# Hybrid decoder block on one core: the first inputs in single k steps behind products on constants, and sums of squares and cumulative sums as high and low parts in f32r

## The chip, the cores and the metric

One core of one Trainium2 chip runs the kernel: TensorE (matrix products), VectorE (DVE), ScalarE (ACT) and SyncE (SP), which issues the transfers. The metric is the device time in microseconds (us); before, the median of three runs is 1462.24 us (1460.91 to 1462.55).

## The reference

One layer of a hybrid decoder, for 256 positions (T) and a width of 2048 (D), all in float32. Cut to what matters:

```python
u = rmsnorm(h, g_mix_pre)                      # x * rsqrt(mean(x*x) + 1e-6) * g
proj = u @ w_in                                # q,k,v of 12 + 4 heads, two gates of width D
ya = dilated_mixture_attention(qa, ka, va) @ w_branch_a
yb = stick_breaking_attention(qb, kb, vb) @ w_branch_b
mix = (sigmoid(gla) * ya + sigmoid(glb) * yb) @ w_out
h = h + rmsnorm(mix, g_mix_post)
up = causal_depthwise_conv(rmsnorm(h, g_ffn_pre) @ w_up, conv_w, conv_b)
f = (gelu(up[:, :5632]) * up[:, 5632:]) @ w_down
h = h + rmsnorm(f, g_ffn_post)
out = h + sigmoid(h @ w_ple_gate) * (p @ w_ple_in)
```

Stick-breaking attention weighs key s for query t by `exp(z + ln + after)`, where `ln = log_sigmoid(-z)` and `after` is the sum of `ln` over the keys between s and t: an exclusive cumulative sum over up to 256 keys.

## The kernel before

Activations are held transposed: 16 tiles (k = 0 to 15) of 128 channels by 256 positions. The weights are packed on the host into one stream of tiles of 128x1024, eight blocks of 128x128 each, in the order in which TensorE uses them. A tile is loaded (`raw`, `NRAW` = 5 buffers), copied by ScalarE to f32r (`hi`, L147) and subtracted by VectorE (`lo` = `raw` - `hi`, L150); activations are split in the same way (`usplit`, `ulow`: the high part beside the low part in one tile of 512 columns). A block is then a pair of products in f32r (`mul`): the high weights by both parts (512 columns, L226), and the low weights by the high part (256 columns, L228). Sums and attention use plain f32 products.

`tick` runs once a tile: it issues deferred work (evacuations, squares), the copies of the tiles ahead (`high`, as far as `at["look"]` says) and the splits and further loads (`lows`). Each engine works in the order in which the program was written. All loads go through SP's queue; a load waits until its buffer's split (L150) is done.

What the change and the steps of the prediction touch:

- **The start.** The first group has four columns and takes k one after the other, so a k step needs one tile of x (128 KB) and half a weight tile (256 KB). The first two steps come singly, the rest of x by twos and the weights in whole tiles. Five weight tiles, w0 to w4, are asked for among x; w4 holds k = 8 and 9.
- **The norms of x and h** (`begin`). The products are not normalised: the norm's factor R is applied when a column is evacuated. Squares are summed beside the first six columns; then `total` multiplies the two sums by ones in f32 (L363), and `rstd` makes R.
- **Cumulative sums** (L520 to L522): ones-triangle `tri` and `allone` by `l1` in f32, once for each of the four head slots s.
- **The turns.** After the output projection (turn 0) and after the down projection (turn 1) the next projection needs h, and so R, first. `square_sum` adds the last column's square and splits the sum for two f32r products (L666), which stand after six of 16 blocks of the small e projection; the other ten blocks run while `rstd` makes R. Then h is updated by two tiles at a time: `scale` (times R, L674), `add` (to h, L678, and the high part on ScalarE), `rest` (the low parts). TensorE's first product of a step waits for the high part, and from the second step on for the low part too.

Of the kernel before, what the change touches and what calls it, by code (L numbers as in the profile page):

```python
# [14 lines left out]
T = 256  # L15
# [11 lines left out]
NRAW = 5  # L27
NSPL = 7
FIRST = 4
LATE = 2  # L30
SETTLE = dict(even=8, turned=9)
# [62 lines left out]
def hybrid_block_kernel(ctx: ExitStack, tc: tile.TileContext, gx, pT, convp, bias, masks, w, out):  # L94
# [161 lines left out]
    def mm(key, src, fn=mul, ps=None, even=0, turned=None):  # L256
# [110 lines left out]
    Rq = ab.tile([128, T], F32, name="Rq")  # L367
    mk = ab.tile([128, 5, 128], F32, name="mk")
    ident, keep01, neg, tri, allone = (mk[:, n] for n in range(5))
# [5 lines left out]
    parts = [(0, 1), (1, 2)] + [(k, k + 2) for k in range(2, KT, 2)]  # L375
    pieces = [[(0, NB // 2), (NB // 2, NB)], [(NB, 2 * NB)]]
    for n, (a, b) in enumerate(parts):
        o = 4 * KT if a else 0
        nc.sync.dma_start(gh[:, o + a * T:4 * KT + b * T], gx[:, o + a * T:4 * KT + b * T])
        if n < 2:  # L380
            for c, d in pieces[n]:
                load(0, c, d)
        elif a * NB // 1024 < NRAW:
            load(a * NB // 1024)
    at["load"] = NRAW
    DVE.memset(f(ones), 1.0)
    DVE.memset(eps32, EPS)
# [13 lines left out]
    usplit(u, 2, h[:, 2], gain(0, 2))  # L401
    at["high"] = at["low"] = 1
    at["look"] = 1
    for c, k, first, last in todo:
        if k == 6:
            at["grow"] = 0.5
        if c == 0 and 0 < k < KT - 2:
# [5 lines left out]
    nc.sync.dma_start(mk, masks)  # L413
    nc.sync.dma_start(cw, convp)

    def begin(pool, spare, keys, pss, src, act_src, name="sum"):
# [7 lines left out]
        pr = pool.tile([128, 2 * T], F32, name=name)  # L424
        total(pr, sq[:, 0], sq[:, 1])
        rstd(pr)

    def qk_evac(s, c, ps):
        def then(sum_to):
            st, r = (Q, Rq) if c < 4 else (K, R)  # L430
# [6 lines left out]
    begin(pat, spare, keys, pss, u, h, "z")  # L437
    DVE.tensor_scalar(Rq, R, 1.0 / math.sqrt(DH), None, op0=OP.mult)
    for c, ps in enumerate(pss):
        qk_evac(0, c, ps)  # L440
    for c in range(len(pss), 8):
        ps = mm(keys[c], u, ps=spare.pop(0) if spare else None)
# [28 lines left out]
    def attention(s):  # L471
# [31 lines left out]
        for c in (0, 256):  # L503
            DVE.tensor_tensor(l1[:, c:c + 128], l1[:, c:c + 128], keep01, OP.mult)
        yield
# [126 lines left out]
    def square_sum(last):  # L632

        sqs = tmp.tile([128, 2 * T], F32R, name="sqs", tag="s2", bufs=2)
        DVE.tensor_tensor(sq[:, 0], sq[:, 0], sq[:, 1], OP.add)
        s2 = square(last)
        DVE.tensor_tensor(sq[:, 0], sq[:, 0], s2, OP.add)
        ACT.activation(sqs[:, :T], sq[:, 0], AF.Copy)
# [237 lines left out]
```

## Time and profile before

| | |
|---|---|
| median of three runs | 1462.24 us |
| profiled execution | 1461.69 us |
| its span, from the first to the last instruction | 1459.9 us |
| TensorE busy | 1448.8 us, 99% of the span |
| VectorE busy, ScalarE busy | 1029.3 us (71%), 811.6 us (56%) |
| DMA engines, mean rate over the span | 60%, 188 GB/s |

A product's busy time runs over the next one's start, since products are pipelined; the step from one start to the next is what a product costs. The page's row of the clock granted to TensorE says 9 tenths or more in all 40 slices. In the rows further down "x4" puts together rows of the same instruction; an f32 product is recorded as two of them. What stands in brackets is the engine's idle time ahead of the instruction, and who ended it.

### The profile page before, as it was taken

The numbers are of one execution on the slowest core, as the hardware profiler recorded it, in microseconds if no ns is written. First come the engines' busy times: TensorE is split into PE (matmuls) and PEld (weight loads), VectorE is DVE, ScalarE is ACT, GpSimd is POOL, SyncE is SP. The second block draws the span as 40 slices with busy tenths as digits, with TensorE's granted clock in tenths as the row PEclk, the third lists the DMA queues.
The fourth block names the chain that finished last, engine by engine and source line by source line (L and its number), as shares of the span: only waits on it lengthen the run. The fifth ranks groups of instructions, "written<-read, shape, count | busy, mean of one in ns | idle before, by whom it ended". The sixth has DMA issues, their size and how long they took to land.

```text
span 1459.9 us, 21906 instructions
## 1 busy us (share of the span) xinstructions
PE 1448.8 (99%) x8433; PEld 1279.9 (88%) x8433; DVE 1029.3 (71%) x1533; ACT 811.6 (56%) x1217; POOL 0.2 (0%) x4
## 2 busy tenths in 40 slices
PE   8999999999999999999999999999999999999998
PEld 7888888889989998988888888888888888888888
DVE  7665555566666665698975787767877678778784
ACT  7463535365555456566754556545655456567562
POOL 0000000000000000000000000000000000000000
PEclk9999999999999999999999999999999999999999
DMA  8645555556666666635766666666666666666381
GB/s 325 223 155 181 171 192 169 193 176 194 188 188 188 188 188 188 221 126 169 214 208 189 189 189 196 189 188 189 188 192 194 190 188 188 189 195 209 114 264 54
DMA packets 78295, 275.11 MB, mean 188 GB/s; under 512 B 8688, under 2 KB 11632, under 8 KB 78192
## 3 DMA queue, kind: packets, MB, share of 16 engines
q1 hardware_dynamic: 78192, 273.73, 60.0%
q8 instruction: 66, 1.08, 0.3%
q14 instruction: 37, 0.30, 0.1%
HBM read 271.60 MB, written 2.10 MB: 187 GB/s over the span
## 4 chain that ended last, share of the span: by engine, by line
PE 98%; DVE 1%; DMA 0%; ACT 0%; SPq 0%; issue 0%
PE mm L226 55%; PE mm L228 29%; PE mm L464 2%; PE mm L462 2%; PE mm L463 2%; PE mm L247 2%; PE mm L246 2%; PE mm L245 2%; PE S L481 1%; PE S L226 1%; DMA raw<-in_w 0%; PE po L535 0%; PE S L515 0%; PE S L228 0%; PE po L226 0%; PE po L539 0%
## 5 line engine op out<-in xcount | busy, mean ns | idle before, releaser
L226 PE MATMUL mm<-u,hi 128*128 128x512 f32 x2596 | 906.2, 393 | 1.4 <-DVE u L318 1.4
L150 DVE TENSOR_TENSOR lo<-raw,hi 128x1024 fp32r<-128x1024 f32 (+1 forms) x506 | 613.3, 1218 | 173.6 <-ACT hi L147 166.1
L228 PE MATMUL mm<-u,lo 128*128 128x256 f32 x2578 | 722.3, 280 | 0.4 <-DVE lo L150 0.4
L147 ACT ACTIVATE hi<-raw 128x1024 fp32r<-128x1024 f32 (+1 forms) x506 | 530.7, 1053 | 244.2 <-PE mm L226 197.6
L226 PEld LDWEIGHTS mm<-u,hi 128*128 128x128 f32 x2596 | 485.8, 188 | 107.1 <-issue 1.6
L228 PEld LDWEIGHTS mm<-u,lo 128*128 128x128 f32 x2578 | 488.0, 189 | 1.8 <-DVE lo L150 0.9
L226 PE MATMUL mm<-ft,hi 128*128 128x512 f32 x693 | 240.4, 391 | 0.0
L273 ACT ACTIVATE t<-mm 128x256 f32<-128x256 f32 x242 | 91.4, 378 | 237.8 <-PE mm L228 237.5
L228 PE MATMUL mm<-ft,lo 128*128 128x256 f32 x693 | 194.0, 280 | 0.0
L276 DVE TENSOR_TENSOR s<-mm,t 128x256 f32<-128x256 f32 x211 | 88.9, 421 | 123.1 <-ACT t L273 123.1
L226 PEld LDWEIGHTS mm<-ft,hi 128*128 128x128 f32 x693 | 129.6, 187 | 28.4
L228 PEld LDWEIGHTS mm<-ft,lo 128*128 128x128 f32 x693 | 131.0, 189 | 0.0
L226 PE MATMUL mm<-mg,hi 128*128 128x512 f32 x240 | 83.2, 391 | 0.0
L228 PE MATMUL mm<-mg,lo 128*128 128x256 f32 x239 | 66.9, 280 | 0.0
L742 ACT ACTIVATE cv<-cpad,cw 128x256 f32<-128x256 f32 x88 | 52.6, 597 | 10.4 <-DVE cpad L737 10.2
L226 PEld LDWEIGHTS mm<-mg,hi 128*128 128x128 f32 x240 | 44.8, 187 | 9.7
L462 PE MATMUL mm<-hi,u 128*128 128x512 f32 x128 | 51.2, 400 | 0.0
L464 PE MATMUL mm<-hi,u 128*128 128x512 f32 x128 | 50.0, 391 | 0.0
L463 PE MATMUL mm<-lo,u 128*128 128x512 f32 x128 | 49.8, 389 | 0.0
L228 PEld LDWEIGHTS mm<-mg,lo 128*128 128x128 f32 x239 | 45.2, 189 | 0.0
L746 DVE SCALAR_TENSOR_TENSOR cv<-cpad,cw,cv 128x256 f32<-128x256 f32 x88 | 42.6, 485 | 3.1
L745 DVE SCALAR_TENSOR_TENSOR cv<-cpad,cw,cv 128x256 f32<-128x256 f32 x88 | 42.1, 478 | 0.0
(183 smaller groups left out, 1003.0 us busy)
## 6 DMA issues: line engine op xcount, KB each, us to landing
raw<-in_w SPq DMA_DIRECT2D x507, 512.0 KB, 3.7
bi<-in_bias SPq DMA_DIRECT2D x4, 576.0 KB, 4.6
out<-t SPq DMA_DIRECT2D x16, 128.0 KB, 3.8
gh<-in_gx SPq DMA_DIRECT2D x7, 256.0 KB, 7.0
mk<-in_masks SPq DMA_DIRECT2D x1, 320.0 KB, 5.2
raw<-in_w SPq DMA_DIRECT2D x2, 128.0 KB, 2.5
raw<-in_w SPq DMA_DIRECT2D x1, 256.0 KB, 4.1
t<-in_pT SPq DMA_DIRECT2D x2, 128.0 KB, 5.0
```

The lines of the kernel that those rows point to most:

```text
L147: ACT.activation(hi[i][:, a:b], raw[i][:, a:b], AF.Copy)
L150: DVE.tensor_tensor(lo[i][:, a:b], raw[i][:, a:b], f(hi[i][:, a:b]), OP.subtract)
L226: PE.matmul(ps, wh, rhs, start=first, stop=last, skip_group_check=True)
L228: PE.matmul(ps[:, :T], wl, rhs[:, :T], start=False, stop=last, skip_group_check=True)
L273: ACT.activation(t1[0], ps[:, T:], AF.Copy)
L276: DVE.tensor_tensor(out, ps[:, :T], t1[0], OP.add)
L462: PE.matmul(pv[t], xh, wh, start=kt == 0, stop=False)
L463: PE.matmul(pv[t], xh, wl, start=False, stop=False)
L464: PE.matmul(pv[t], xl, wh, start=False, stop=kt == KT - 1)
L742: ACT.activation(y, c[:, 2:], AF.Identity, scale=cw[:, n, 2:3], bias=cw[:, n, 3:4])
L745: DVE.scalar_tensor_tensor(y, c[:, 1:T + 1], cw[:, n, 1:2], y, op0=OP.mult, op1=OP.add)
L746: DVE.scalar_tensor_tensor(y, c[:, 0:T], cw[:, n, 0:1], y, op0=OP.mult, op1=OP.add)
```

## The change

1. **Start.** x and the weights of the first eight k steps come in pieces of one step (`EARLY` = 8), each piece split as it comes; then x by twos, and only then w4. Raw buffers are four instead of five. Six f32 products of 128 columns on a tile of ones (`WARM` = 6), into a bank that nothing reads, stand ahead of TensorE's first product, and the two fills of constants come ahead of the loads.
2. **Sums of squares.** All go through `halves`: a copy to f32r on ScalarE and a subtraction on VectorE, and `total` is then two f32r products. In `begin`, sum and `rstd` move from the end of the sixth column to after three blocks of the seventh (`mid`).
3. **Cumulative sums.** `l1` is split in the same way (`l2`), `tri` is copied to f32r, and the products are two of 384 columns and two of 128.
4. **Turns.** The sum is in two parts: squares of columns 0 to 14 (after three blocks of e) and of column 15 (after five in turn 0, after six in turn 1). The first of these is added and split ahead of `lows`, which stood first before. The first two tiles of h are scaled and added one by one, and their low parts come ahead of the next tiles' scaling.

On SP's queue the start reads so before (L379 loads x, L119 weights; the first x transfer has the gains in it, 512 columns of x are two k steps and 1024 columns of weights are one tile):

```order
L379 DMA gh<-in_gx 128x320
L119 DMA raw<-in_w 128x256 x2
L379 DMA gh<-in_gx 128x256
L119 DMA raw<-in_w 128x512
L379 DMA gh<-in_gx 128x512
L119 DMA raw<-in_w 128x1024
L379 DMA gh<-in_gx 128x512
L119 DMA raw<-in_w 128x1024
L379 DMA gh<-in_gx 128x512
L119 DMA raw<-in_w 128x1024
L379 DMA gh<-in_gx 128x512
L119 DMA raw<-in_w 128x1024
```

After it come three more of x, and then weights. Now, from step 5 on (the rows of steps 1 to 4 repeat in pairs):

```order
L400 DMA gh<-in_gx 128x256
L121 DMA raw<-in_w 128x512
L400 DMA gh<-in_gx 128x256
L121 DMA raw<-in_w 128x512
L400 DMA gh<-in_gx 128x256
L121 DMA raw<-in_w 128x512
L400 DMA gh<-in_gx 128x512 x4
L121 DMA raw<-in_w 128x1024 x9
```

The first five transfers are the same; w4, fifth of the whole tiles before and ahead of x's last three transfers, is now the first of the nine that stand behind all of x.

On VectorE, at the end of the down projection (turn 1), before (L150 splits a weight tile, L331 adds a square, L784 adds the last column, L635 to L639 make the sum and its low part, L674 scales, L678 adds to h):

```order
L150 TENSOR_TENSOR lo<-raw,hi 128x1024
L331 TENSOR_TENSOR sq<-sq,t 128x256
L784 TENSOR_TENSOR ff<-ff,mm 128x256
L635 TENSOR_TENSOR sq<-sq 128x256
L637 TENSOR_TENSOR sq<-sq,t 128x256
L639 TENSOR_TENSOR sqs<-sq,sqs 128x256
L353 TENSOR_SCALAR ms<-sum 128x256
```

and now (L336 adds a square, L379 and L369 make the first sum and its low part, L152 splits the weight tile, L817 adds the last column, L369 makes its square's low part):

```order
L336 TENSOR_TENSOR sq<-sq,t 128x256
L379 TENSOR_TENSOR sq<-sq 128x256
L369 TENSOR_TENSOR sp<-sq,sp 128x256
L152 TENSOR_TENSOR lo<-raw,hi 128x1024
L817 TENSOR_TENSOR ff<-ff,mm 128x256
L369 TENSOR_TENSOR sp<-t,sp 128x256
L358 TENSOR_SCALAR ms<-sum 128x256
```

The weight tile's split has moved from ahead of the last square's add to behind it and the two new operations; the last column's add still follows it.

The same engine after R in turn 1, before:

```order
L674 TENSOR_TENSOR ts<-ff,R 128x512
L678 TENSOR_TENSOR gh<-gh,ts 128x512
L674 TENSOR_TENSOR ts<-ff,R 128x512
L316 TENSOR_TENSOR u_12682<-gh,u_12682 128x256 x2
L678 TENSOR_TENSOR gh<-gh,ts 128x512
```

and now (L708 and L709 are the same on one tile, L321 the low parts):

```order
L708 TENSOR_TENSOR ts<-ff,R 128x256
L709 TENSOR_TENSOR gh<-gh,ts 128x256
L708 TENSOR_TENSOR ts<-ff,R 128x256
L709 TENSOR_TENSOR gh<-gh,ts 128x256
L321 TENSOR_TENSOR u_12730<-gh,u_12730 128x256 x2
L700 TENSOR_TENSOR ts<-ff,R 128x512
L704 TENSOR_TENSOR gh<-gh,ts 128x512
```

The first tile is ready for its high part after two short operations instead of two long ones, and the low parts (x2) stand ahead of the next scaling instead of behind it.

The diff, cut to its core:

```diff
-NRAW = 5
+NRAW = 4
+EARLY = 8
+WARM = 6
...
         for n, (_, k, first, last) in enumerate(group(key)):
+            if n == 3 and mid:
+                mid()
...
-    def total(ps, *accs, start=True, stop=True):
-        for n, acc in enumerate(accs):
-            PE.matmul(ps[:, :T], f(ones), acc, start=start and n == 0, stop=stop and n == len(accs) - 1)
+    def halves(src):
+        sp = tmp.tile([128, 2 * T], F32R, name="sp", tag="s2", bufs=2)
+        ACT.activation(sp[:, :T], src, AF.Copy)
+        DVE.tensor_tensor(sp[:, T:], src, f(sp[:, :T]), OP.subtract)
+        return sp
+    def total(ps, sp, start=True, stop=True):
+        for n in range(2):
+            PE.matmul(ps[:, :T], ones, sp[:, n * T:(n + 1) * T], start=start and n == 0, stop=stop and n == 1)
+    def sum_squares():
+        DVE.tensor_tensor(sq[:, 0], sq[:, 0], sq[:, 1], OP.add)
+        return halves(sq[:, 0])
...
-    parts = [(0, 1), (1, 2)] + [(k, k + 2) for k in range(2, KT, 2)]
-    pieces = [[(0, NB // 2), (NB // 2, NB)], [(NB, 2 * NB)]]
+    parts = [(k, k + 1) for k in range(EARLY)] + [(k, k + 2) for k in range(EARLY, KT, 2)]
+    pieces = {k: [(k // 2, k % 2 * NB + c, k % 2 * NB + d)
+                  for c, d in ([(0, NB // 2), (NB // 2, NB)] if k == 0 else [(0, NB)])] for k in range(EARLY)}
...
+    for _ in range(WARM):
+        PE.matmul(spare[2][:, :128], f(ones), f(ones), start=True, stop=True)
-    for k in range(2):
+    for k in range(EARLY):
         usplit(u, k, h[:, k], gain(0, k), low=False)
-        for c, d in pieces[k]:
-            high(0, c, d)
-            low(0, c, d)
-        ulow(u, k, h[:, k], gain(0, k))
+        k and ulow(u, k, h[:, k], gain(0, k))
+        for piece in pieces[k]:
+            high(*piece)
+            low(*piece)
+        k or ulow(u, k, h[:, k], gain(0, k))
...
-        PE.matmul(ps[:, 0:256], tri, l1[:, 0:256], start=True, stop=False, skip_group_check=True)
-        PE.matmul(ps[:, 128:256], allone, l1[:, 256:384], start=False, stop=True, skip_group_check=True)
-        PE.matmul(ps[:, 256:384], tri, l1[:, 256:384], start=False, stop=True, skip_group_check=True)
+        for c in range(2):
+            PE.matmul(ps[:, :384], tri, l2[:, c], start=c == 0, stop=c == 1, skip_group_check=True)
+        for c in range(2):
+            PE.matmul(ps[:, 128:256], ones, l2[:, c, 256:], start=False, stop=c == 1, skip_group_check=True)
...
     ps = mm(("down", NQ - 1, KT - 1), ft, mul1)
+    flush()
+    sps = [sum_squares()]
     lows(at["high"])
-    flush()
     DVE.tensor_tensor(ff[:, KT - 1], ff[:, KT - 1], ps[:, :T], OP.add)
-    sqs = square_sum(ff[:, KT - 1])
+    sps.append(halves(square(ff[:, KT - 1])))
...
-            if i == 5:
-                for c in range(2):
-                    PE.matmul(pr[:, :T], ones, sqs[:, c * T:(c + 1) * T], start=c == 0, stop=c == 1)
+            if i in (2, 4 + half):
+                total(pr, sps[i > 2], i == 2, i > 2)
...
         def add(n):
-            DVE.tensor_tensor(h[:, k:k + 2], h[:, k:k + 2], ts.pop(n), OP.add)
+            if n:
+                DVE.tensor_tensor(h[:, 2 * n:2 * n + 2], h[:, 2 * n:2 * n + 2], ts[n], OP.add)
+            for j in range(2):
+                k = 2 * n + j
+                if n == 0:
+                    DVE.tensor_tensor(ts[0][:, j], src[:, k], R, OP.mult)
+                    DVE.tensor_tensor(h[:, k], h[:, k], ts[0][:, j], OP.add)
                 usplit(dst, k, h[:, k], gn[k], low=False)
...
         add(0)
+        rest(0)
         scale(1)
-        rest(0)
         add(1)
```

## Rows read from the trace of the kernel before

**Rows 1.** The page: the chain that ended last, by engine.

```profile
PE 98%; DVE 1%; DMA 0%; ACT 0%; SPq 0%; issue 0%
```

**Rows 2.** Timeline of the first 22 us, TensorE: start us, us, engine, line, operation.

```profile
3.90 0.58 PE L235 MATMUL mm<-u,hi 128*128 128x256 f32 x1 [3.90 <-ACT hi L147]
...
9.40 0.63 PE L226 MATMUL mm<-u,hi 128*128 128x512 f32 x1
...
10.04 0.63 PE L226 MATMUL mm<-u,hi 128*128 128x512 f32 x1
...
13.87 0.40 PE L226 MATMUL mm<-u,hi 128*128 128x512 f32 x1
...
14.22 0.40 PE L226 MATMUL mm<-u,hi 128*128 128x512 f32 x1
...
21.29 0.40 PE L226 MATMUL mm<-u,hi 128*128 128x512 f32 x1
```

**Rows 3.** Start: VectorE, ScalarE (same columns), SP's waits, the page's weight loads.

```profile
7.39 0.69 DVE L150 TENSOR_TENSOR lo<-raw,hi 128x512 fp32r<-128x512 f32 x1 [1.67 <-ACT hi L147]
...
9.97 1.06 ACT L147 ACTIVATE hi<-raw 128x1024 fp32r<-128x1024 f32 x1 [0.89 <-DMA raw<-in_w]
...
18.88 1.06 ACT L147 ACTIVATE hi<-raw 128x1024 fp32r<-128x1024 f32 x1 [1.32 <-DMA raw<-in_w]
...
19.98 1.23 DVE L150 TENSOR_TENSOR lo<-raw,hi 128x1024 fp32r<-128x1024 f32 x1 [1.11 <-ACT hi L147]
...
SPq L119 <- DMA raw<-in_w: 2.2, 3, 0.9
...
raw<-in_w SPq DMA_DIRECT2D x507, 512.0 KB, 3.7
```

**Rows 4.** The chain in order of time, sums of squares: start us, us.

```profile
44.07 0.86 PE z L363 x4
...
621.33 0.25 PE sum L666 x2
```

**Rows 5.** Timeline, the first cumulative sum: start us, us.

```profile
103.84 0.59 PE L520 MATMUL z<-l,mk 128*128 128x256 f32 x2
...
104.27 0.38 PE L521 MATMUL z<-l,mk 128*128 128x128 f32 x2
...
104.49 0.39 PE L522 MATMUL z<-l,mk 128*128 128x128 f32 x2
```

**Rows 6.** Timeline of turn 0.

```profile
623.94 0.69 DVE L674 TENSOR_TENSOR ts<-mix,R 128x512 f32<-128x512 f32 x1
...
625.95 0.39 PE L235 MATMUL mm<-u,hi 128*128 128x256 f32 x1 [0.79 <-ACT u L310]
...
628.00 0.89 DVE L318 SCALAR_TENSOR_TENSOR u<-gh,u 128x256 fp32r<-128x256 f32 x2
...
628.90 0.39 PE L226 MATMUL mm<-u,hi 128*128 128x512 f32 x1
```

**Rows 7.** Timeline of turn 1.

```profile
1357.70 1.23 DVE L150 TENSOR_TENSOR lo<-raw,hi 128x1024 fp32r<-128x1024 f32 x1 [0.44 <-ACT hi L147]
...
1357.97 0.40 ACT L322 ACTIVATE t<-ff 128x256 f32<-128x256 f32 x1
...
1358.84 0.42 DVE L331 TENSOR_TENSOR sq<-sq,t 128x256 f32<-128x256 f32 x1
...
1359.61 0.42 DVE L784 TENSOR_TENSOR ff<-ff,mm 128x256 f32<-128x256 f32 x1 [0.35 <-PE mm L247]
...
1360.07 0.42 ACT L322 ACTIVATE t<-ff 128x256 f32<-128x256 f32 x1 [1.15 <-DVE ff L784]
...
1361.42 0.42 DVE L639 TENSOR_TENSOR sqs<-sq,sqs 128x256 fp32r<-128x256 f32 x1 [0.48 <-ACT sqs L638]
...
1366.58 0.39 PE L235 MATMUL mm<-u,hi 128*128 128x256 f32 x1 [0.70 <-ACT u L310]
...
1369.54 0.39 PE L226 MATMUL mm<-u,hi 128*128 128x512 f32 x1
```

More of the change, by code (lines that the diff above doesn't have):

```diff
@@ L374, in hybrid_block_kernel @@
     NB = FIRST * 128
-    parts = [(0, 1), (1, 2)] + [(k, k + 2) for k in range(2, KT, 2)]
-    pieces = [[(0, NB // 2), (NB // 2, NB)], [(NB, 2 * NB)]]
-    for n, (a, b) in enumerate(parts):
+    parts = [(k, k + 1) for k in range(EARLY)] + [(k, k + 2) for k in range(EARLY, KT, 2)]
+    pieces = {k: [(k // 2, k % 2 * NB + c, k % 2 * NB + d)
+                  for c, d in ([(0, NB // 2), (NB // 2, NB)] if k == 0 else [(0, NB)])] for k in range(EARLY)}
+    DVE.memset(f(ones), 1.0)
+    DVE.memset(eps32, EPS)
+    for a, b in parts:
         o = 4 * KT if a else 0
         nc.sync.dma_start(gh[:, o + a * T:4 * KT + b * T], gx[:, o + a * T:4 * KT + b * T])
-        if n < 2:
-            for c, d in pieces[n]:
-                load(0, c, d)
+        if a < EARLY:
+            for piece in pieces[a]:
+                load(*piece)
         elif a * NB // 1024 < NRAW:
@@ L413, in hybrid_block_kernel, with begin @@
     nc.sync.dma_start(mk, masks)
+    defer((None, None), (None, None), (lambda: ACT.activation(tri, mk[:, 3], AF.Copy), None))
     nc.sync.dma_start(cw, convp)
-    def begin(pool, spare, keys, pss, src, act_src, name="sum"):
+    def begin(pool, spare, keys, pss, src, act_src, then, name="sum"):
         at["grow"] = 1
@@ L423, in begin, with mid @@
         flush()
-        pr = pool.tile([128, 2 * T], F32, name=name)
-        total(pr, sq[:, 0], sq[:, 1])
-        rstd(pr)
+        sp = sum_squares()
+        def mid():
+            pr = pool.tile([128, 2 * T], F32, name=name)
+            total(pr, sp)
+            rstd(pr)
+            then()
+        return mid
     def qk_evac(s, c, ps):
         def then(sum_to):
-            st, r = (Q, Rq) if c < 4 else (K, R)
+            st, r = (Q, Rs[1]) if c < 4 else (K, R)
             if c % 4 == 0:
@@ L436, in hybrid_block_kernel, with then @@
     keys = [("qk", 0, c) for c in range(8)]
[L437 to L440, printed above, removed]
+    def then():
+        Rs.append(tmp.tile([128, T], F32, name="Rq", tag="y"))
+        DVE.tensor_scalar(Rs[1], R, 1.0 / math.sqrt(DH), None, op0=OP.mult)
+        for c, ps in enumerate(pss):
+            qk_evac(0, c, ps)
+    mid = begin(pat, spare, keys, pss, u, h, then, "z")
     for c in range(len(pss), 8):
-        ps = mm(keys[c], u, ps=spare.pop(0) if spare else None)
+        ps = mm(keys[c], u, ps=spare.pop(0) if spare else None, mid=mid if c == len(pss) else None)
         qk_evac(0, c, ps)
@@ L630, in scaled @@
         return lambda: ACT.activation(src[:, j], src[:, j], AF.Copy, scale=gain(gi, j)), None
[L632 to L638, printed above, removed]
-        DVE.tensor_tensor(sqs[:, T:], sq[:, 0], f(sqs[:, :T]), OP.subtract)
-        return sqs
     for j, ps in enumerate(several("out", 3, mg, 1)):
@@ L646, in hybrid_block_kernel @@
     ps = mm(("out", KT - 1), mg, mul1)
+    flush()
+    sps = [sum_squares()]
     lows(at["high"])
-    flush()
-    sqs = square_sum(ps[:, :T])
+    sps.append(halves(square(ps[:, :T])))
     DVE.tensor_scalar(mix[:, KT - 1], ps[:, :T], gain(1, KT - 1), None, op0=OP.mult)
@@ L652, in hybrid_block_kernel, with turn @@
     fp_sc, fp = scope("fp")
-    def turn(half, edst, sqs, src, gnext, dst, nxt):
+    def turn(half, edst, sps, src, gnext, dst, nxt):
         at["hold"] = True
@@ L846, in _arrays @@
     a["masks"] = np.ascontiguousarray(np.stack([
-        i == j, i < j, np.where(i < j, 0.0, NEG), i >= j, np.ones((128, 128))], 1).astype(np.float32))
+        i == j, i < j, np.where(i < j, 0.0, NEG), i >= j], 1).astype(np.float32))
     ws = {"w_in": w_in[0], "w_branch_a": w_branch_a[0], "w_branch_b": w_branch_b[0], "w_out": w_out[0],
```

42 lines of the change are left out of this document (22 added, 20 removed).

## The prediction

> **What bounds the kernel now.** I read the page's chain of waits first [rows 1]: 98% of that chain is TensorE itself. So the time is the sum of TensorE's products plus the few places where it stands still or runs slowly, and a change is worth only what it does to these. VectorE and ScalarE matter where TensorE waits for them: in the first 22 us, and in the two "turns", where a layer norm stands between two projections.
>
> Then the timeline of the first 30 us. A pair of products (512 and 256 columns) starts every 0.64 us at 9.40 and 10.04, but every 0.35 us at 13.87 and 14.22 [rows 2]. The page's clock row says full clock in every slice, so the level is read from the spacing: 1.2 GHz until about 13.4 us, 2.4 GHz after it, with TensorE at work since 3.9 us but with pauses. The ninth step of the first group (k = 8) starts at 21.29.
>
> Then the chain and timeline at the sums and cumulative sums [rows 4, 5], and around the two turns [rows 6, 7].
>
> **The change part by part.** Durations are of the profiled execution, which took 1461.69 us, of which 1459.9 are the span; the median of the three runs, 1462.24, is 0.55 us higher. What I sum goes on 1461.69; a median needs 0.55 more.
>
> *Start.* New are six products on constants before the data is there, and x and the weights in pieces of one k step for the first eight steps. The products on constants have no other reader, and before's TensorE is idle until 3.9 us [rows 2], so they cost nothing as long as they end by then: six f32 products of 128 columns at twice the 0.22 us of one at full clock [rows 5] are 2.6 us from about 1.0, so until 3.6. What they give is an earlier rise of the clock. How much of it reaches the end is decided by the fifth weight tile (w4, for k = 8). Before, it was asked for ahead of half of x. Now SP asks for w4 behind all of x and four tiles, so it lands with the 4640 KiB that x, the gains and five tiles make up. Before, 1568 KiB were there at 9.97 and 5152 KiB at 18.88, the two places where ScalarE waited for a transfer [rows 3]: 3584 KiB in 8.91 us, 402 KiB per us. 4640 KiB are there at 18.88 - 512/402 = 17.6, if the smaller pieces come at the same rate; I take 18.0 (estimate, a little for the shorter rows). From landing to the low part VectorE starts 1.10 us later and takes 1.23 [rows 3]: 20.35, so the first low product of k = 8 starts at 20.4. Before, it follows the one at 21.29 by 0.23, at 21.52. That is 1.1 us. The products before it are not later than that: the second step cannot start before about 8.1 us (it needs the same first five transfers, and before its split runs from 7.39 for 0.69 [rows 3]), and 28 pairs from there end at 17.9 at 0.35, and at 20.3 if the clock rises only at 13.4. So the clock's rise is largely hidden behind w4: TensorE gets to k = 8 early and waits there. Bounds of this term: 0 if w4 lands at 19.1, and 3.4 if nothing but TensorE counts (17.9 against 21.29). I take 1.1, from the nearest row.
>
> *Sums of squares.* Two f32 products of 256 columns take 0.86 us at the first of two such sums, and the second is alike; the same in f32r take 0.25 [rows 4]. Twice 0.61 is 1.2 us gained. New are an add, a copy and a subtraction, at 0.46 us a step [rows 7] some 1.4 us; they lie beside the products of the running column, and the sum now waits until three pairs (1.06 us) of the next column are through. If that cover were gone TensorE would wait 0.3 us.
>
> *Cumulative sums*, one per s, four in all. Before: 0.43 + 0.22 + 0.22 = 0.87 us [rows 5]. After: two products of 384 columns and two of 128 in f32r. 256 columns take 0.12 [rows 4], 512 take 0.35 - 0.12 = 0.23 [rows 2], so 384 take 0.175. A narrow f32r product is in no row. The bounds are 0.06 (half of 256) and 0.22 (the f32 product of 128 columns); nearest is the f32r one of 256, so I take 0.12. That is 0.35 + 0.24 = 0.59, a gain of 0.28, four times 1.1 us; by the bounds 0.3 to 1.6. The copy and the subtraction that split the operand lie beside the products of one attention step, several us before they are read.
>
> *First turn* (0, after the output projection). R comes 0.12 us earlier, since the final sum moves one block of three products (0.36) ahead and one pair of sums (0.24) comes in front of it. Tile 0 is now scaled, added and split by halves, so the first product can start 0.65 us earlier than 625.95 [rows 6]: the wait of 0.79 us nearly goes. But the same VectorE now does four operations of 256 where two of 512 stood, at steps of 0.46 where one needs the last one's result and 0.34 where not (0.42 less the 0.09 by which VectorE starts ahead of an end, as 1358.84 follows 1357.70 with its 1.23 [rows 7]) against 0.69 each, and does the low parts of tile 0 ahead of the next scaling. The low part that k = 2 needs started at 628.00 and now starts at about 628.4, while TensorE would be there at 628.25; with 0.5 us from there to the product it starts at 628.94, against 628.90. The wait is moved, not removed: 0, with bounds of 0.6 us gained and 0.3 lost.
>
> *Second turn* (1, after the down projection). Here an order changes for the worse. Before, VectorE splits the last weight tile at 1357.70, while it waits for ScalarE's square of 1357.97, and is free when the last column of the projection arrives at 1359.61 [rows 7]. Now the square's add, the new add and the new subtraction stand ahead of that 1.23 us split, and the last column's add stands behind it. Steps: add of the square 1358.39, sum 1358.85, copy on ScalarE 1359.31, subtraction 1359.76, split 1360.10, and 1.14 later (1357.70 to 1358.84) the last column's add, 1361.24 instead of 1359.61. From there square, copy and subtraction (0.46, 0.44, 0.45; one step fewer than before) end the chain with a subtraction at 1362.59, against 1361.42: R is 1.17 us later. The halves of tile 0 give 0.5 back, so the first product is at 1367.2 instead of 1366.58; and as in the first turn the low part for k = 2 is the next thing late, at 1370.3, its product at 1370.75 instead of 1369.54. That is a loss of 1.2 us, with bounds of 0.5 and 1.7.
>
> *Four raw buffers instead of five.* A tile takes 3.7 us to land, 1.06 to copy and 1.23 to split [rows 3], 6.0 us; four buffers cover four tiles of eight pairs, 11.3 us. Nothing, unless transfers take over 9 us.
>
> Sum: -1.1 - 1.2 - 1.1 + 0 + 1.2 = -2.2 us: 1459.5 on the profiled execution's time, 1460.0 as a median. A measurement of this kernel can tell about 0.2%, 2.9 us, from no change, so this is no change, with a lean towards faster.
>
> **The rivals.**
> 1. The start is bounded by TensorE: transfers keep up, w4 is there by 17.9. For it: the fast rate comes only after 8 us, and before's tiles were there before they were needed. Against it: 4640 KiB in all must be there, and w4 is the last of them. Start -3.4, the rest as above: -4.5, so 1457.7.
> 2. Smaller pieces come slowly (the other side). SP waited for the landing of earlier transfers before it issued new ones [rows 3], so the number in flight is limited; pieces half as large put half the bytes in flight. If the rate goes with the size, the twelve pieces of steps 2 to 7 (2304 KiB) at 201 KiB per us take 11.5 us from 6.7 (0.7 ahead of the split at 7.39), to 18.2, and x's rest with w4 (1536 KiB at 402) 3.8, to 22.0; the first low product of k = 8 is at 24.4, 2.9 us later than before. Sum +1.8, so 1464.0. The start loses from where w4 lands after 19.1, and from 20.2 on the whole is slower. Against it: half the bytes in flight are still 1.5 MiB, nearly 4 us of the measured rate.
> The Trainium skill, "DMA: Bandwidth & Descriptors", section Measured, speaks for this rival: it advises batching to 1 MiB or more for three quarters of the peak, with 138 GB/s at 64 KB and 341 at 1 MB. No run here shows a long row of 128 and 256 KB transfers, so it is not borne out yet.
> 3. The second turn is not delayed: the split of the last tile finds a gap, or TensorE's remaining products of that stretch cover it. Then the halves are worth what they are meant to be: 0 instead of +1.2, so -3.4 and 1458.8. Against it: VectorE works in order, and the split stands ahead of the add in its program.
>
> **How the numbers follow.** My forecast 0.53 (own range 1458.9 to 1461.6), rival 1 0.18, rival 2 0.10, rival 3 0.19. Faster by over 0.2% are rival 1, most of rival 3 and the low edge of mine (narrow products at 0.06, w4 at 17.6): 0.37. Slower by over 0.2% is only the far end of rival 2: 0.04. Within 0.2%: 0.59. The range runs from rival 1 to just past no change: 1457.6 to 1462.5.
>
> **What would show it.** Start: the first low product of k = 8 at 20.4, TensorE idle ahead of it, and pairs at 0.35 well before 13.4. If k = 8 starts at 18, rival 1; after 21.5, rival 2. Sums: two products at 0.25. Cumulative sums: z at 0.59 in place of 0.87; at 0.79 the narrow ones go at the f32 price. First turn: first product near 625.3 on before's scale, then a pause before k = 2. Second turn: a weight split on VectorE between the halves and the last column's add, the second pair of sums waiting some 1.2 us, and pauses before k = 0 and k = 2. I am wrong if the second turn is no later than before, or if the time is under 1457.6 or over 1462.5.

## The result, and the profile after

The changed kernel takes 1465.49 us (median of ten runs, 1464.17 to 1465.82); the kernel before, run beside it, 1461.34 (1460.85 to 1462.55). The ratio is 1.0025, with a 95% interval of 1.0016 to 1.0035. It is slower by about 4 us where I had forecast 1460.0 and a lean towards faster; on 1461.34 instead of 1462.24 that forecast would have been 0.9 lower still. The profiled execution took 1465.45 us with a span of 1463.6, 3.7 more than before's.

To see where these 3.7 us arise I set each of the 3577 products of L226 (512 columns, now L228) against the same product in the trace of before and followed the difference in their starts. It is -1.6 us at 41.8, +3.9 at 52.6 (just behind the first sum), +2.0 at 311 (behind the four cumulative sums), +2.3 behind the first turn, +1.8 behind the second sum, +3.0 behind the second turn and +3.5 from 1395 to the end. One place, the first sum, lost 5.6 us. All else together gained 2.0, of which the four cumulative sums are 1.4.

The page's chain of waits is TensorE's as before, one point less [rows 1], and one point in 100 is over 14 us, so it can't show a loss of this size:

```profile
PE 97%; DVE 1%; DMA 1%; ACT 1%; SPq 0%; issue 0%; DVEq 0%; ACTq 0%
```

**The start**, TensorE in the timeline (start us, us, engine, line, operation, idle time ahead of it and what ended it), answering to [rows 2]:

```profile
1.04 2.93 PE L415 MATMUL po<-ones 128*128 128x128 f32 x12 [1.04 <-DVE epsb L397]
...
8.15 0.39 PE L228 MATMUL mm<-u,hi 128*128 128x512 f32 x1
...
8.50 0.40 PE L228 MATMUL mm<-u,hi 128*128 128x512 f32 x1
...
18.89 0.50 PE L228 MATMUL mm<-u,hi 128*128 128x512 f32 x1 [1.04 <-ACT hi L149]
20.15 0.38 PE L230 MATMUL mm<-u,lo 128*128 128x256 f32 x1 [0.76 <-DVE lo L152]
```

The clock is up at 8 us (pairs 0.35 apart, where before had 0.64 until 13.4), yet the ninth step starts only at 18.89 and its first low product at 20.15: TensorE waits for the fifth weight tile, which ScalarE starts to copy when it lands (answering to [rows 3]):

```profile
17.78 1.06 ACT L149 ACTIVATE hi<-raw 128x1024 fp32r<-128x1024 f32 x1 [3.26 <-DMA raw<-in_w]
```

The rate at which the pieces came, from windows of before and of after (us, length, busy time of TensorE, of its weight loads, of VectorE, ScalarE and GpSimd, granted clock, DMA share, GB/s):

```profile
8.00:10.00 2.00, 1.38 (x4) 1.22 (x5) 0.96 (x3) 0.53 (x2) 0.00 (x0) 1.00 0.95 370
```

```profile
8.00:10.00 2.00, 2.00 (x12) 1.77 (x13) 1.83 (x4) 1.76 (x4) 0.00 (x0) 1.00 0.98 301
```

The smaller pieces run at 301 GB/s against 370: somewhat slower, far from the half rate that the rival on the other side needed. The clock column says 1.00 in both, although before's pairs are 0.64 apart there: its trace has no record of the granted clock ahead of 13.7 us (4.6 in the changed kernel's), so at the start the level is read from the spacing of the pairs.

**The first sum.** ScalarE and VectorE in the timeline of after: the copy that waits for its tile, the mask's job, the last add of squares and the start of the new chain:

```profile
36.28 1.06 ACT L149 ACTIVATE hi<-raw 128x1024 fp32r<-128x1024 f32 x1 [2.22 <-DMA raw<-in_w]
37.24 0.29 ACT L436 ACTIVATE tri<-mk 128x128 fp32r<-128x128 f32 x1
...
43.97 1.49 DVE L350 TENSOR_TENSOR sq<-sq,s 128x512 f32<-128x512 f32 x2 [0.30 <-ACT s L345]
45.49 0.42 DVE L379 TENSOR_TENSOR sq<-sq 128x256 f32<-128x256 f32 x1
46.30 0.42 ACT L368 ACTIVATE sp<-sq 128x256 fp32r<-128x256 f32 x1 [1.85 <-DVE sq L379]
```

The same last add of squares in the timeline of before:

```profile
38.27 1.48 DVE L345 TENSOR_TENSOR sq<-sq,s 128x512 f32<-128x512 f32 x2
```

It ended at 39.75 there and ends at 45.46 now, 5.7 us later. Before, 4.3 us were to spare until TensorE's sum at 44.07 [rows 4]. TensorE now, and the windows behind it:

```profile
43.14 0.28 PE L230 MATMUL po<-u,lo 128*128 128x256 f32 x1
46.77 1.04 PE L375 MATMUL z<-sp,ones 128*128 128x256 f32 x2 [3.35 <-ACT sp L368]
47.61 0.63 PE L228 MATMUL po<-u,hi 128*128 128x512 f32 x1
...
48.25 0.63 PE L228 MATMUL po<-u,hi 128*128 128x512 f32 x1
```

```profile
47.00:52.00 5.00, 5.00 (x16) 4.15 (x17) 4.87 (x10) 3.00 (x6) 0.00 (x0) 0.50 0.43 140
52.00:57.00 5.00, 5.00 (x31) 4.43 (x30) 3.51 (x8) 1.50 (x3) 0.00 (x0) 0.96 0.53 175
```

Two losses, one behind the other: TensorE stands still for 3.35 us, and then the granted clock is 0.50, so that pairs are 0.64 us apart from 47.6 to 52.1. A window that is 100% busy can still be half speed: 16 products in 5 us against 31 in the next.

**The other places**, all TensorE or VectorE in the timeline of after: a cumulative sum, the first turn, the second sum and the second turn, answering to [rows 5 to 7]:

```profile
107.75 0.51 PE L555 MATMUL z<-l,tri 128*128 128x384 f32 x2
108.10 0.34 PE L557 MATMUL z<-l,ones 128*128 128x128 f32 x2
108.27 0.45 PE L228 MATMUL mm<-u,hi 128*128 128x512 f32 x1
...
631.18 0.50 PE L228 MATMUL mm<-u,hi 128*128 128x512 f32 x1 [0.59 <-DVE u L323]
...
662.86 0.40 PE L375 MATMUL sum<-sp,ones 128*128 128x256 f32 x2
663.10 0.28 PE L247 MATMUL mm<-u,hi 128*128 128x256 f32 x1
...
1361.88 1.22 DVE L152 TENSOR_TENSOR lo<-raw,hi 128x1024 fp32r<-128x1024 f32 x1
1363.01 0.41 DVE L817 TENSOR_TENSOR ff<-ff,mm 128x256 f32<-128x256 f32 x1
...
1364.38 0.84 PE L375 MATMUL sum<-sp,ones 128*128 128x256 f32 x2 [0.65 <-ACT sp L368]
...
1372.57 0.50 PE L228 MATMUL mm<-u,hi 128*128 128x512 f32 x1 [0.41 <-DVE u L321]
```

A cumulative sum takes 0.52 us (107.75 to 108.27) instead of 0.87; the second sum 0.24 without a wait; the first turn pauses ahead of k = 2 instead of k = 0; in the second the weight split stands at 1361.88, between the halves and the last column's add, as forecast.

### The profile page after: what moved, and what is told of

Read it like the earlier page. It is cut to its first block, busy times and chain, and to the rows that moved or that the text cites. A ratio compares the mean times of both kernels' runs of the same rounds, so it can differ in the third digit from the quotient of the medians.

```text
span 1463.6 us, 21957 instructions
## 1 busy us (share of the span) xinstructions
PE 1450.2 (99%) x8437; PEld 1280.0 (87%) x8437; DVE 1035.5 (71%) x1548; ACT 818.1 (56%) x1229; POOL 0.2 (0%) x4
## 4 chain that ended last, share of the span: by engine, by line
PE 97%; DVE 1%; DMA 1%; ACT 1%; SPq 0%; issue 0%; DVEq 0%; ACTq 0%
PE mm L228 55%; PE mm L230 28%; PE mm L495 2%; PE mm L493 2%; PE mm L494 2%; PE mm L248 2%; PE mm L249 1%; PE mm L247 1%; DMA raw<-in_w 1%; PE S L512 1%; PE S L228 0%; PE po L570 0%; PE po L228 0%; PE S L549 0%; PE S L230 0%; ACT hi L149 0%
## 5 line engine op out<-in xcount | busy, mean ns | idle before, releaser
L228 PE MATMUL mm<-u,hi 128*128 128x512 f32 x2596 | 904.4, 393 | 3.0 <-ACT hi L149 2.0
L152 DVE TENSOR_TENSOR lo<-raw,hi 128x1024 fp32r<-128x1024 f32 (+2 forms) x509 | 614.4, 1212 | 178.1 <-ACT hi L149 168.8
L149 ACT ACTIVATE hi<-raw 128x1024 fp32r<-128x1024 f32 (+2 forms) x509 | 532.2, 1049 | 257.7 <-PE mm L228 198.4
L228 PEld LDWEIGHTS mm<-u,hi 128*128 128x128 f32 x2596 | 484.8, 187 | 109.3 <-ACT hi L149 2.5
L228 PE MATMUL mm<-ft,hi 128*128 128x512 f32 x693 | 240.4, 391 | 0.0
L228 PEld LDWEIGHTS mm<-ft,hi 128*128 128x128 f32 x693 | 129.6, 187 | 28.4
L228 PE MATMUL mm<-mg,hi 128*128 128x512 f32 x240 | 83.2, 391 | 0.0
L772 ACT ACTIVATE cv<-cpad,cw 128x256 f32<-128x256 f32 x88 | 52.6, 598 | 8.1 <-DVE cpad L767 7.8
L228 PEld LDWEIGHTS mm<-mg,hi 128*128 128x128 f32 x240 | 44.8, 187 | 9.7
```

Of the source, the lines that this page charges most:

```text
L149: ACT.activation(hi[i][:, a:b], raw[i][:, a:b], AF.Copy)
L152: DVE.tensor_tensor(lo[i][:, a:b], raw[i][:, a:b], f(hi[i][:, a:b]), OP.subtract)
L228: PE.matmul(ps, wh, rhs, start=first, stop=last, skip_group_check=True)
L772: ACT.activation(y, c[:, 2:], AF.Identity, scale=cw[:, n, 2:3], bias=cw[:, n, 3:4])
```

## The experiments

The intervals are of the ratio to the kernel before, run on the same chip. Experiments 1 to 4, 5 to 8, 9 and 10, and 11 ran on four chips; the kernel before took 1461.28, 1461.16, 1461.18 and 1460.88 us on them.

**1. The mask's conversion out of the queue.** `defer((None, None), (None, None), (tri...))` goes, and behind the first projections' table load comes:

```diff
+    ACT.activation(tri, mk[:, 3], AF.Copy)
```

> The conversion of the triangular mask to f32r is taken out of the queue of deferred jobs, where it stands one place ahead of the four stages of squares, and is done once after the first projections instead. Nothing else changes. Theory A (the queue hands out one new job per weight tile, so the mask's job delays every stage of the squares by one tile, 2.8 us, and the last stage falls behind the last tile): the squares end some 5 us earlier, the halves of the first sum are ready before TensorE reads them at about 43.3 us, its wait of 3.35 us and the half clock after it go, and the time falls by about 5.4 us, to about 1460.1. Theory B (four raw buffers hold ScalarE up at a weight tile for 2.2 us, and that delay is what the sum waits for): the squares still stand behind the blocked copy, the wait stays at 2.5 to 3.3 us and the time at 1464.5 to 1465.5. Theory C (three pairs of products, 1.06 us, are too little cover for the chain add, copy, subtraction, whenever it starts): the wait shrinks to the 0.5 us that the chain of 1.5 us has over its cover, the clock may still fall, and the time is 1461 to 1465.

Measured: 1461.19 us, ratio 1.0004 (0.9995 to 1.0012). There is no wait at the sum, and the median falls by 4.3 of the 5.4 us of theory A. The trace supports A less than this sounds. It is of an execution of 1463.10 us, in which TensorE waited 1.68 and 0.76 us at the ninth step and then ran at half clock (window of this kernel, columns as above):

```profile
20.00:25.00 5.00, 4.08 (x14) 3.29 (x15) 4.86 (x7) 5.00 (x10) 0.00 (x0) 0.66 0.66 215
```

So TensorE itself came late to the sum:

```profile
42.95 1.48 DVE L350 TENSOR_TENSOR sq<-sq,s 128x512 f32<-128x512 f32 x2
...
46.26 0.40 PE L375 MATMUL z<-sp,ones 128*128 128x256 f32 x2
```

The last add of squares ends at 44.43, 1.0 us earlier than in the changed kernel and not the 5 that A expected; TensorE begins the sum at 46.26, where the changed kernel's was ready at 43.42. What the job's place costs has to be read from experiments 5 and 11. The time lies in theory C's range as well; against C speaks experiment 5, where the halves are complete at 42.69, ahead of TensorE at 43.12.

**2. Five raw buffers.**

```diff
-NRAW = 4
+NRAW = 5
-        l2 = ab.tile([128, 2, 384], F32R, name="l2")
+        l2 = [tmp.tile([128, 2 * T], F32R, name="l2", tag="s2", bufs=2) for _ in range(2)]
```

> Five raw weight buffers instead of four; the split operand of the cumulative sums goes into two tiles that the squares' pool has free at that time, which makes the room. Theory B (ScalarE blocked on a tile that four buffers ask for too late): the copy of the tile that started after a wait of 2.22 us at 36.28 starts 2 us earlier, the last squares too, the wait of 3.35 us at the first sum falls to about 1.2, and the time by 2 to 5 us, depending on whether the clock still falls. Theory A (one tile's delay by the mask's job): the last stage of the squares comes behind the last tile as before, the wait is 2.5 to 3.3 us, the time within 1 us of 1465.5.

Measured: 1460.88 us, ratio 1.0001 (0.9992 to 1.0009). TensorE in its timeline:

```profile
18.44 0.39 PE L230 MATMUL mm<-u,lo 128*128 128x256 f32 x1 [0.29 <-DVE lo L152]
...
43.57 0.84 PE L375 MATMUL z<-sp,ones 128*128 128x256 f32 x2 [1.09 <-ACT sp L368]
44.26 0.39 PE L228 MATMUL po<-u,hi 128*128 128x512 f32 x1
...
44.60 0.40 PE L228 MATMUL po<-u,hi 128*128 128x512 f32 x1
```

Theory B holds too: the wait falls from 3.35 to 1.09, the pairs behind it are 0.35 apart, and the last add of squares ends at 42.24, 3.2 us earlier. The first low product of the ninth step is 1.7 us earlier too: with five buffers SP asks for the fifth tile at 10.07 us, ahead of x's last three transfers, and with four at 11.83, right behind them. A alone, which gave this run nothing, falls.

**3. Both sums 11 pairs later.**

```diff
-            if n == 3 and mid:
+            if n == 14 and mid:
```

> Both sums behind the first six columns are placed after 14 pairs of the next column instead of 3. All theories of the lateness of the halves agree: 11 pairs more are 3.85 us of cover, more than the wait of 3.35 us, so TensorE does not stand still at 43.3 us. What this run prices is the stall with all that hangs on it: if the half clock of 6.8 us behind the idle time is caused by that idle time, the time falls by 5.4 us, to about 1460.1; if the clock falls in any case (its cause being the products or the chip), only by 3.3, to 1462.1. If R, now 3.85 us later, holds up the evacuation of the first six columns so that the next columns want for a bank, TensorE waits there instead and less is gained.

Measured: 1482.28 us (1471.00 to 1486.56), ratio 1.0134 (1.0107 to 1.0161). The wait at the sum is gone and at 45.8 us this trace is 6.3 us ahead, as all theories had it; but it cannot price the stall, since R is late for its own readers:

```profile
52.28 0.44 PE L478 MATMUL z<-mk,R 128*128 128x128 f32 x2 [3.90 <-DVE R L363]
...
671.47 0.76 PE L228 MATMUL mm<-u,hi 128*128 128x512 f32 x1 [2.56 <-DVE s L281]
...
672.25 0.63 PE L228 MATMUL mm<-u,hi 128*128 128x512 f32 x1
```

The transposes of R wait 3.90 us, behind the second sum a column waits 2.56 for a bank to be read out, and half clock follows each. Most of the 17 us came as a surprise, and from elsewhere: this trace is 6.9 us behind the changed kernel's at 690 us and 19.6 behind at 1360 (experiment 8).

**4. The wait filled with products.** 28 f32r products on constants ahead of the first sum (`for _ in range(28): PE.matmul(pr[:, T:], ones, src[:, 0, :T], ...)`).

> 28 f32r products of 256 columns on constants stand ahead of the first sum, in the other half of its bank, which nobody reads: 3.3 us at 0.118 each, about as long as TensorE waits there for the halves. The sum is not earlier for it. Theory idle (the clock falls because TensorE stood still for 3.5 us): the clock stays full, the products from 47 to 52 us run at 0.35 us a pair instead of 0.64, and the time falls by 2.9 to 3.4 us, to about 1462.3. Rival (the clock falls for another reason, such as the narrow f32r sum or what the other engines do): it falls as before and the time stays at 1465.5.

Measured: 1464.73 us, ratio 1.0024 (1.0015 to 1.0034).

```profile
44.72 3.51 PE L453 MATMUL z<-u,ones 128*128 128x256 f32 x28
48.07 0.40 PE L375 MATMUL z<-sp,ones 128*128 128x256 f32 x2
48.31 0.40 PE L228 MATMUL po<-u,hi 128*128 128x512 f32 x1
...
48.66 0.40 PE L228 MATMUL po<-u,hi 128*128 128x512 f32 x1
```

The clock stays full behind the sum, so the fall in the changed kernel does hang on TensorE's standing still. The Trainium skill, "TensorE: Matmul & The Clock Gate", section "Why this matters for your kernels", warns of idle gaps between bursts of products for this reason; the trace agrees, at 3.35 us. From just ahead of the sum to the pair at 52.59 us of the changed kernel's trace this one gains 2.9 us, as expected. The medians differ by only 0.8. This profile lost 1.6 us at the ninth step, where waits of 0.95 and 0.76 us were followed by half clock (0.50 from 21 to 24 us), and 1.0 near its end; what keeps the median from the 1462.3 expected is not shown.

**5. Experiments 1 and 2 together.**

> The mask's conversion out of the queue and five raw buffers together. With five buffers alone the fifth weight tile came earlier too (its first low product at 18.7 us, where the changed kernel had 20.15) and a wait of 1.09 us was left at the first sum; with the mask's job out alone there was no wait at the sum, but the changed kernel's late fifth tile, with a half clock behind it in that trace. Theory (two separate delays, each of about one tile, that add up in the changed kernel): no wait at the first sum, first low product of the ninth step at 18.7, no half clock; the time is 1.0 to 2.5 us below either alone, 1458.5 to 1460. Rival (one delay, which either edit takes away in full): the time of either alone, 1460.9 to 1461.2.

Measured: 1459.51 us, ratio 0.9988 (0.9980 to 0.9997). In its trace the sum at 43.12 us follows the pair before it without a wait. That is 1.4 us below five buffers alone and 1.7 below the job's edit alone, so neither takes the whole delay away; the intervals overlap by 0.0005 and 0.0002. The last add of squares ends at 41.25, still 1.5 later than before the change. The ninth step's low product is at 19.23, not 18.7.

**6. The weight split first, on top of 5.**

```diff
+    lows(at["high"])
     flush()
     sps = [sum_squares()]
-    lows(at["high"])
```

> As the kernel with both edits, and at both turns the split of the last weight tile on VectorE stands ahead of the flush and the sum of squares again, as in the kernel before the change. Theory (the step of the prediction: behind the halves, that split holds up the last column's add by 1.2 us): the second turn's first product comes 0.9 to 1.3 us earlier, the first turn's within 0.3 us, and the time falls by about 1.2 us against the kernel with both edits. Rival (the split only changes place: ahead of the halves it delays them, and the halves delay the last column's add by as much): no change within 0.3 us, since VectorE has the same work between the same two events.

Measured: 1458.54 us, ratio 0.9981 (0.9972 to 0.9990). VectorE in the second turn:

```profile
1353.44 1.22 DVE L152 TENSOR_TENSOR lo<-raw,hi 128x1024 fp32r<-128x1024 f32 x1 [0.44 <-ACT hi L149]
...
1355.95 0.42 DVE L369 TENSOR_TENSOR sp<-sq,sp 128x256 fp32r<-128x256 f32 x1 [0.48 <-ACT sp L368]
1356.29 0.42 DVE L817 TENSOR_TENSOR ff<-ff,mm 128x256 f32<-128x256 f32 x1
```

The split fills the time in which VectorE waited for ScalarE's square, and the last column's add follows the halves at once. Relative to the stretch before the turn its first product (1362.35, for 1363.79 in experiment 5's trace, which was 0.75 later already) comes 0.7 us earlier, against 0.9 to 1.3 expected: the theory holds in kind, not wholly in size, as the halves still stand ahead of the last column's add. The first turn moved by less than 0.2. The median falls by 1.0, but the intervals of 5 and 6 overlap, so the gain rests on the traces; these end 2.5 apart, as in experiment 5's the slower rhythm of experiment 8 lasts from the second turn to the end.

**7. No products on constants** (`WARM = 0` in the changed kernel).

> The changed kernel without the six products on constants at the start. Theory (the early clock is hidden behind the fifth weight tile, as predicted): the products of the first eight steps run at half clock up to 13 us, TensorE reaches the ninth step at 20 to 21 us instead of 18, where it waited for that tile until 20.15 anyway, and the time stays within 0.6 us of 1465.5. Rival (without them the clock rises later than in the kernel before, since the pieces come singly with pauses between): 28 pairs at 0.64 us from 8 us end at 26, the time is 1469 to 1471.

Measured: 1466.66 us, ratio 1.0036 (1.0023 to 1.0050), an interval that overlaps the changed kernel's.

```profile
8.32 0.39 PE L228 MATMUL mm<-u,hi 128*128 128x512 f32 x1
...
8.67 0.40 PE L228 MATMUL mm<-u,hi 128*128 128x512 f32 x1
```

The pairs are 0.35 apart from 8.3 us without them, so the early clock does not need these products. Nor is it shown to come from the pieces: experiment 10 has them and a late clock, experiment 11 has whole tiles and an early one. That the early clock gains nothing by itself is not what this run could test, since the clock was early all the same.

**8. Equal products once more behind experiment 3's second sum.**

```diff
-            ps = mm(keys[n], u2, **dict(SETTLE, mid=mid) if n == len(pss) else {})
+            ps = mm(keys[n], u2, **dict(SETTLE, mid=mid) if n == len(pss) else SETTLE if n == len(pss) + 2 else {})
```

> The kernel with both sums 11 pairs later took 1482 us: in its trace every three pairs of products took 349 + 350 + 361 ns from the second sum on to the second turn, where the changed kernel has 346 + 347 + 347. Here, in addition, the third column after that sum begins with eight steps in three products of 256 columns each, as the first column after the sum does already. Theory (a rhythm of TensorE alone, into which the stall behind the sum put it, and which a stretch of equal products sets back): from that column on three pairs take 1.040 us again, and the time falls by some 12 to 16 us, to 1466 to 1470. Rival (something outside TensorE's own stream slows it, such as the transfers or the other engines): the rhythm stays at 1.060 us and the time at 1482.

Measured: 1471.06 us (1468.06 to 1484.44), ratio 1.0081 (1.0049 to 1.0112). Windows of experiment 3, then of this one:

```profile
700.00:800.00 100.00, 100.00 (x568) 86.77 (x567) 76.19 (x120) 57.41 (x89) 0.00 (x0) 1.00 0.63 191
```

```profile
700.00:800.00 100.00, 100.00 (x579) 88.19 (x578) 77.02 (x120) 58.31 (x90) 0.00 (x0) 1.00 0.63 197
```

TensorE is 100% busy at clock 1.00 in both, with 568 against 579 products. The time is close to the theory's, but the trace does not show the theory's cause. TensorE just ahead of the added steps, and the first of these:

```profile
675.65 0.39 PE L228 MATMUL mm<-u,hi 128*128 128x512 f32 x1
...
676.69 0.39 PE L228 MATMUL mm<-u,hi 128*128 128x512 f32 x1
...
679.11 0.28 PE L247 MATMUL mm<-u,hi 128*128 128x256 f32 x1
```

Three pairs take 1.04 us already here (675.65 to 676.69), and the added steps begin at 679.11: behind this stall the faster rhythm came up without them. The runs point the same way. Of experiment 3's six, one took 1471.00 us and five 1480.85 to 1486.56; of this kernel's five, four took 1468.06 to 1472.21 and one 1484.44. Which rhythm comes up seems to differ from run to run, and whether the added steps change the odds is open. The Trainium skill, "Perfetto Trace Analysis", section "Identifying the Most-Contended Engine", says that the busy share of products is no measure of how near TensorE is to its limit and advises, among others, the weight loads' share; the trace agrees (100.00 twice for the products, 86.77 and 88.19 for the weight loads).

**9. Equal products in more places, on top of 6** (at the head of the fifth column behind each first group and of every other column of the s = 1 to 3 projections).

> The kernel with both edits and the split first (1458.5 us), and eight steps in three products of 256 columns, as before only after each turn, also at the head of the fifth column behind each first group and of every other column of the twelve-score projections (s = 1 to 3). In the trace without them three pairs take 1.060 us from 22.6 to 42, in much of the columns between 101 and 305, and from 625 to 655 us. Theory (equal products set the rhythm back for as long as nothing makes TensorE stand): these stretches go at 1.040 us for three pairs after the eight steps; about 20 + 150 + 60 pairs at 6.7 ns each are 1.5 us less, 1457.0. Rival (the rhythm is picked anew at each of the attention's products between the pairs, so that it holds only where nothing stands between, and eight steps cost what they give): within 0.5 us of 1458.5.

Measured: 1460.05 us, ratio 0.9991 (0.9982 to 1.0000): 1.5 above 6, with intervals that overlap. Ahead of the first added steps three pairs take 349 + 350 + 361 ns (24 to 29.5 us), behind them 346 + 347 + 347 (34 to 41 us), where 6's trace keeps the slower rhythm until 41.7. So equal products can set the rhythm back, and as the edit touches nothing but TensorE's stream, the rhythm can be changed from there alone. But the attention's products change it again within a column or two: from 41 to 310 us this trace loses 0.8 us on 6's, and after 1380 us 1.1 more, in the slower rhythm. The theory's gain did not come; the rival is nearer, if too kind.

**10. No products on constants, on top of 6.**

> The kernel with both edits and the split first (1458.5 us), without the six products on constants. In the changed kernel their absence moved the time by about 1 us at most: there the clock rose by 8 us without them, and the fifth tile was waited for in any case. Here that tile comes with the ninth step's turn (its first low product at 18.69, TensorE there at 18.2), so a late clock would show. Theory (the pieces alone keep TensorE busy enough for the early clock): pairs at 0.35 us from 8 us, 1458.5 within 0.7. Rival (the products on constants give the early clock where TensorE waits a little longer for its first data): the clock rises at 10 to 13 us in this kernel, k = 8 comes up to 3 us later, the time is 1460 to 1461.5.

Measured: 1458.25 us, ratio 0.9982 (0.9973 to 0.9990), the same as 6. In this trace the clock did rise late (pairs 0.64 apart from 8.98 to 11.5), against the theory's mechanism; yet of the 1.6 us so lost only 1.1 were left at 23 us, and 0.7 at the end. This supports that a late clock is partly hidden behind the transfers.

**11. The two delays alone, in the kernel before.**

```diff
-NRAW = 5
+NRAW = 4
+    defer((None, None), (None, None), (None, None))
```

> The kernel before the change with nothing but the two delays: four raw buffers instead of five, and an empty job in the queue where the changed kernel has the mask's conversion. There the last add of squares ended at 39.75 and TensorE began the first sum at 44.07, so 4.3 us were to spare; the empty job takes one tile (2.8 us), the blocked copy up to 2.2. Theory (the delays add and were the greater part of the changed kernel's stall; with neither the halves nor the earlier start that asks for them sooner they just use up what was spare): the last add ends between 42.6 and 44.8, TensorE waits 0 to 0.8 us at the first sum, without a half clock, and the time is within 1 us of 1461.2. Rival (the delays alone stall TensorE by several us, and the halves have no part in it): a wait of over 2 us, half clock behind it, 1464 to 1466.

Measured: 1463.86 us, ratio 1.0020 (1.0011 to 1.0029).

```profile
43.68 1.49 DVE L345 TENSOR_TENSOR sq<-sq,s 128x512 f32<-128x512 f32 x2 [0.94 <-ACT s L340]
...
45.22 2.08 PE L363 MATMUL z<-sq,ones 128*128 128x256 f32 x4 [2.97 <-DVE sq L345]
```

My theory fell: the last add ends at 45.17 (5.4 us later than before, more than I allowed), TensorE waits 2.97 us, and the granted clock is 0.50 from 45 to 48 us. Wait and half clock are the rival's; its time, 1464 to 1466, is just missed. So the delays, without the halves, already cost 3.0 us. In this trace TensorE was ready for the sum 1.8 us earlier than in before's (pairs 0.35 apart from 8.96 us, with neither pieces nor products on constants), which made the wait longer.

The first sum in the traces, from their rows (us; the sum's start in the kernel before is that of [rows 4]):

| trace | last add of squares ends | sum begins | wait ahead of it |
|---|---|---|---|
| before | 39.75 | 44.07 | none |
| changed | 45.46 | 46.77 | 3.35 |
| 1, job out | 44.43 | 46.26 | none |
| 2, five buffers | 42.24 | 43.57 | 1.09 |
| 5, both | 41.25 | 43.12 | none |
| 6, both and split first | 40.14 | 42.37 | none |
| 11, delays alone | 45.17 | 45.22 | 2.97 |

## Why the prediction was wrong

- **The failed step** is the cover of the first sum: "they lie beside the products of the running column ... If that cover were gone TensorE would wait 0.3 us." I took the moment at which the squares are complete from the trace of before and put only the new chain behind it. Two other edits of the same change moved that moment. The account from rows: 4.3 us were to spare before; the last add ends 5.7 later, TensorE is there 0.65 earlier (43.42 for 44.07), and from that add's end to the first product are 1.3: 5.7 + 0.65 + 1.3 - 4.3 = 3.35, the wait in the trace. Experiments 5 and 11 show that the two delays are most of the 5.7: without both the add ends 4.2 us earlier, and both alone, put into the kernel before, make it 5.4 later. How they divide it is not shown: five buffers alone give 3.2 of it back, the job's edit alone 1.0, in a trace in which TensorE was late itself. The half clock behind the wait, which experiment 4 ties to it, made it 5.6 us net where I had booked a gain of 0.6. That is the miss: all other parts together came to -2.0, for -1.6 forecast.
- **The first delay** I missed: the queue hands out one job per weight tile, and the mask's job stands ahead of the squares. I read the job as a copy on ScalarE of a fraction of a microsecond and did not ask what stands behind it in the queue.
- **The second** I booked as "Nothing, unless transfers take over 9 us." The two transfers of the page that stand in SP's queue ahead of a needed tile take 6.6 us each, where the median tile takes 3.7:

```profile
mk<-in_masks SPq DMA_DIRECT2D x1, 256.0 KB, 6.6
...
cw<-in_convp SPq DMA_DIRECT2D x1, 176.0 KB, 6.6
```

  The tile asked for behind them at 28.98 was there at 36.2, 7.2 us later. That is under my 9, but ScalarE works in order, and the squares stood behind the blocked copy (2.22 us).
- **Start:** right in size and in the wait for the fifth tile. Forecast -1.1 with the low product at 20.4; measured -1.3 at 20.15, and pieces at 301 GB/s did not make the other side's rival. That the pieces and the products on constants made this gain is not shown: experiment 11's trace, which has neither, is 1.8 us ahead of before's at 41 us, the changed kernel's 1.6.
- **Cumulative sums:** right in sign, small in size: 0.35 gained in each, where I took 0.28; the narrow products take 0.085, inside the bounds of 0.06 and 0.22.
- **Second sum:** right: 0.6 gained, as forecast.
- **First turn:** right: the wait moved to k = 2; +0.24 for 0, inside the bounds.
- **Second turn:** right in mechanism and size: +1.27 for +1.2, and experiment 6, which undoes that order, gets 0.7 of it back.
- **Not foreseen:** half a microsecond behind the second turn, from the rhythm of experiment 8.

The kernel of experiment 6 (1458.54 us) beats the kernel before by 0.19% (0.10 to 0.28), and its median lies 0.47% below the changed one's (experiment 10 is its equal): most of the change was worth having, and it was spoilt by where one small job stood, one buffer and, by the traces, one split.

## What to carry to other kernels

When a step is moved closer to its reader, take the time of its inputs from the changed order and not from the old trace: list every edit that touches the queues ahead of it, a job that costs nothing included, because its place can cost a whole round. Edits that are each covered by the same slack have to be summed against that slack once. Where TensorE would stand still, count what its clock does behind the wait as well; here filling the wait with products gave 2.9 us back, beside the wait of 3.35.

## What the runs showed of the hardware

- After the wait of 3.35 us TensorE ran at 1.2 GHz for pairs from 47.6 to 52.1 us; after 2.97 us (experiment 11) the granted clock was 0.50 from 45 to 48 us, and after 1.09 us (experiment 2) it stayed at 1.00. There the sum's two products are 0.46 us apart because the second reads the low half, which VectorE has ready at 43.97.
- Short waits close together went either way: 1.68 and 0.76 us (experiment 1) and 0.95 and 0.76 us (experiment 4) were followed by half clock, 1.04 and 0.76 us (the changed kernel, same place) were not.
- At full clock, with no wait in the trace, three pairs of 512 and 256 columns start either 346 + 347 + 347 or 349 + 350 + 361 ns after one another, for hundreds of us on end. Which of the two holds changed behind a stall (experiments 3 and 8), behind equal products and at the attention's products (experiment 9); over a stretch of 700 us it is worth some 13 us (20 ns in 1040), more than the whole change. What decides it stays open.
